# The whole program ordered by another simulation: timeline simulation in place of core simulation

## The chip, the cores and the metric

The kernel is one program on one core of a Trainium2 chip. The metric is the device time of one execution in microseconds (us), from the start of the program to its end. A core has five engines that run their own instruction lists in order and wait for one another through semaphores: TensorE (PE in the profile, its weight loads PEld), VectorE (DVE), ScalarE (ACT), GpSimd (POOL) and SyncE (SP), which here issues nearly all DMA transfers.

## The reference

The input is x, 256 tokens of 1024 features in float32, and one condition vector c of 1024. Cut to what matters:

```python
for i in range(2):                       # layer 0, layer 1
    shift, scale, gate = split(silu(c) @ ada_w[i] + ada_b[i], 3)
    h = rms_norm(x, norm_g[i]) * (1 + scale) + shift
    y = nsa_mixer(h, ...) if i == 0 else moba_mixer(h, ...)   # 16 heads of 64; (o * silu(z)) @ w_out
    x = x + gate * y
# second block: the same modulation; 8 heads of windowed attention and 8 heads of
# neighbourhood attention side by side, RMS norm of each half, w_out, gate, residual;
# then peer(): a router takes 8 x 16 of 16384 experts for each token,
# gelu(h . u_e) * softmax weight, summed over v_e; residual, final norm
```

## The kernel before

Everything is float32, held to float32 accuracy. A matrix product is written as three passes (`mm3`, L236): the left and right operand are split into a high and a low part, and high by high, high by low and low by high are summed in PSUM. A weight tile of 128x1024 is loaded by a DMA that SP issues (`raw`, four buffers), ScalarE casts each half to its high part (`hi`, L186) and VectorE subtracts to get the low part (`lo`, L211). A few tiles go into other buffers for the same purpose (`mo`).

The stages are: the first part of the modulation (`ada_first`, L350 on, its matmuls at L365); layer 0; layer 1 (both with scores L725, softmax L730 to L745, transposes of the probabilities L701, copies of them out of PSUM L703, products with v L706, and four units `z_unit` that compute the gate z); the second block (`block2`, L1135 on: `heads8` makes scores at L1117 and softmax at L1118 to L1131 for eight heads at once; `o_a` transposes at L1178 and multiplies at L1183, `o_b` at L1200 and L1206); and `peer`, which streams 128 tiles of u and 128 of v, two thirds of the time. `out_half` (L1251) multiplies the gated attention outputs (`ozh`, `ozl`) by w_out. Each layer begins with its norm: a row of small VectorE operations (`rstd_x`, L264) makes one factor for each token, a diagonal matrix of it is multiplied with x (`norm_x`, L517), and the projections follow.

The modulation of the later layers, `ada`, needs no attention at all: five groups a1 to a5 of 16 tiles of 512 KB, each tile two matmuls of 32x512 (L393) into one accumulator `psa`. The tiles have three buffers (`adaw`). These, the z units and the projections are the work that TensorE can do while an attention unit is in its softmax.

The program is written in the order of a string for each layer; `s` is a scores unit, `v` or `oa`/`ob` the transposes and products with v, `z` a gate unit, `a` an ada group, `o` and `O` the two halves of the output projection, and a number after `@` moves the priority of a step:

```python
'1': 'pA@1 q0 s000 s001 v00 q1@-2 s011 s010 v01@-4 z1 s100 z3 s110 s101 z0 z2 b s111 v10@-1 v11@-6 o O',
'2': 'pA@-2 qa@1 sa0 oa0 kb@-1 qb sa1 oa1 vb tb sb0@5 a4 ob0@1 sb1 a5 o ob1 O@5'
...
self.tc.cur_priority += 50 * int(later or 0)
f(*(int(c) for c in s[1:] if c.isdigit()))
self.tc.cur_priority -= 50 * int(later or 0)
```

This is not yet the order on the engines. The framework's scheduler (`TileContext`) simulates the program as it builds it, and gives each engine, among the instructions that are ready at that simulated time, the one of best priority; the buffers of the pools are handed out in the same pass. The resulting list of each engine is fixed in the program: on the chip an engine never overtakes an instruction that waits. For the last stage the code adds ordering of its own (`paced`, L1457).

## Time and profile before

| | |
|---|---|
| three runs | 1412.24, 1414.01, 1414.22 us; median 1414.01 us |
| profiled execution | 1413.74 us, of which the span of the trace is 1412.0 us |
| busy in the span | TensorE 1366.8, VectorE 1023.2, ScalarE 821.9, GpSimd 21.9 us |
| granted TensorE clock | 0.992 of 2.4 GHz on average |

TensorE is busy in 97% of the span. Its busy time contains matmuls that overlap, so groups of matmuls add up to more than the stretch they stand in; what is certain is the time in which it stood idle, about 45 us.

### The profile page before, as it was taken

Reading aid. Unit: us, or ns where it says so; the run is one execution under the profiler, and the core shown is the slowest. Engines: PE = TensorE matmul, PEld = TensorE weight load, DVE = VectorE, ACT = ScalarE, POOL = GpSimd, SP = SyncE. Lnnn points to the kernel's source line nnn. Section 1 sums busy time; section 2 is a strip of 40 time slices with the busy share of each in tenths; the row PEclk is TensorE's granted clock in tenths of the full one; section 3 lists DMA queues with packets and bytes.
Section 4 is the critical chain, followed back from the end, with each engine's and each line's share of the span. In section 5 each row is a group of like instructions: output and inputs, shape, how many; then the busy total and the mean of one; then the engine's idle time right before and its main releaser. Section 6 shows DMA issues by size and latency. Waiting matters only on the chain.

```text
span 1412.0 us, 24444 instructions
## 1 busy us (share of the span) xinstructions
PE 1366.8 (97%) x8522; PEld 1120.8 (79%) x8522; DVE 1023.2 (72%) x2636; ACT 821.9 (58%) x1887; POOL 21.9 (2%) x27
## 2 busy tenths in 40 slices
PE   6999999999989998999999999999999999999997
PEld 2566666477767755999999999999998888888885
DVE  3585756388665656799999968888866666677777
ACT  2353656357646654555555568888865555555554
POOL 0000000000001100000000000000000000000001
PEclk9999999999999999999999999999999999999999
DMA  8577564553486766455555555554456665677773
GB/s 309 199 272 273 197 203 138 199 186 101 138 313 199 216 225 223 135 182 179 179 179 179 181 188 193 165 164 162 165 194 227 194 194 194 194 227 239 245 242 114
DMA packets 94875, 279.15 MB, mean 198 GB/s; under 512 B 11112, under 2 KB 30320, under 8 KB 94624
## 3 DMA queue, kind: packets, MB, share of 16 engines
q1 hardware_dynamic: 94752, 277.59, 59.6%
q8 instruction: 67, 1.10, 0.3%
q14 instruction: 56, 0.46, 0.1%
HBM read 267.80 MB, written 13.94 MB: 200 GB/s over the span
## 4 chain that ended last, share of the span: by engine, by line
PE 90%; DVE 4%; DMA 4%; ACT 1%; issue 1%; SPq 0%; ACTq 0%; DVEq 0%
PE ps L240 18%; PE ps L239 18%; PE ps L241 18%; PE acc L240 5%; PE acc L239 5%; PE acc L241 5%; PE psa L393 5%; PE ps L1493 4%; PE ps L706 2%; DMA raw<-in_w1o 1%; PE ps L725 1%; PE ps L701 1%; PE psa L365 1%; DMA adaw<-in_adaw 1%; DVE lo L211 1%; PE ps L631 1%
## 5 line engine op out<-in xcount | busy, mean ns | idle before, releaser
L186 ACT CAST hi<-raw 128x512 fp32r<-128x512 f32 (+1 forms) x700 | 429.4, 618 | 349.9 <-PE ps L240 147.1
L211 DVE TENSOR_TENSOR lo<-raw,hi 128x512 fp32r<-128x512 f32 (+1 forms) x700 | 479.8, 688 | 179.7 <-ACT hi L186 162.8
L239 PE MATMUL ps<-hh,hi 128*128 128x256 f32 x1160 | 333.0, 287 | 1.3 <-DVE hh L187 1.3
L240 PE MATMUL ps<-hl,hi 128*128 128x256 f32 x1160 | 328.3, 283 | 1.1 <-DVE hl L211 1.1
L241 PE MATMUL ps<-hh,lo 128*128 128x256 f32 x1160 | 328.4, 283 | 0.0
L239 PEld LDWEIGHTS ps<-hh,hi 128*128 128x128 f32 x1160 | 222.6, 192 | 1.5 <-issue 1.5
L240 PEld LDWEIGHTS ps<-hl,hi 128*128 128x128 f32 x1160 | 222.4, 192 | 1.3 <-DVE hl L211 1.3
L241 PEld LDWEIGHTS ps<-hh,lo 128*128 128x128 f32 x1160 | 222.2, 192 | 0.0
L239 PE MATMUL ps<-hi,Ah 128*128 128x512 f32 x508 | 198.1, 390 | 0.0
L240 PE MATMUL ps<-lo,Ah 128*128 128x512 f32 x508 | 197.7, 389 | 0.0
L241 PE MATMUL ps<-hi,Al 128*128 128x512 f32 x508 | 197.6, 389 | 0.0
L239 PEld LDWEIGHTS ps<-hi,Ah 128*128 128x128 f32 x508 | 95.4, 188 | 20.1 <-issue 0.2
L241 PEld LDWEIGHTS ps<-hi,Al 128*128 128x128 f32 x508 | 95.4, 188 | 19.9
L240 PEld LDWEIGHTS ps<-lo,Ah 128*128 128x128 f32 x508 | 95.4, 188 | 19.9 <-DVE lo L211 0.2
L1492 ACT ACTIVATE og<-o,gT 128x128 f32<-128x128 bf16 x256 | 87.2, 394 | 4.1 <-DVE o L1490 0.3
L393 PE MATMUL psa<-adaw,cond 128*32 128x512 f32 x320 | 81.3, 610 | 3.1 <-DMA adaw<-in_adaw 3.1
L240 PE MATMUL acc<-lo,hh 128*128 128x512 f32 (+1 forms) x176 | 70.7, 402 | 2.4 <-DVE lo L211 2.4
L239 PE MATMUL acc<-hi,hh 128*128 128x512 f32 (+1 forms) x176 | 69.6, 401 | 2.6 <-DVE hh L187 1.4
L241 PE MATMUL acc<-hi,hl 128*128 128x512 f32 (+1 forms) x176 | 69.9, 398 | 0.0
L1493 PE MATMUL ps<-og,o 128*128 128x128 f32 x512 | 65.2, 275 | 0.1
L1493 PEld LDWEIGHTS ps<-og,o 128*128 128x128 f32 x512 | 61.4, 192 | 0.3 <-ACT og L1492 0.3
L733 ACT ACTIVATE P<-P,nm 128x128 f32<-128x128 f32 (+1 forms) x96 | 42.6, 446 | 13.5 <-DVE nm L730 13.4
(397 smaller groups left out, 1929.8 us busy)
## 6 DMA issues: line engine op xcount, KB each, us to landing
raw<-in_u SPq DMA_DIRECT2D x128, 512.0 KB, 3.6
raw<-in_v SPq DMA_DIRECT2D x128, 512.0 KB, 4.3
adaw<-in_adaw SPq DMA_DIRECT2D x86, 512.0 KB, 4.9
raw<-in_w SPq DMA_DIRECT2D x48, 512.0 KB, 4.3
raw<-in_wq SPq DMA_DIRECT2D x16, 512.0 KB, 3.4
zd<-ge SPq DMA_DIRECT2D x56, 128.0 KB, 1.7
ge<-zd SPq DMA_DIRECT2D x56, 128.0 KB, 3.6
raw<-in_adaw SPq DMA_DIRECT2D x10, 512.0 KB, 7.0
```

The costliest lines, as they stand in the source:

```text
L186: return self.nc.scalar.copy(out, in_)
L211: return self.nc.vector.tensor_tensor(lo, src, hi.bitcast(F32), op=OP.subtract)
L239: mm(out, a[0][asl], b[0][bsl], start=first, stop=False, **kw)
L240: mm(out, a[0][asl], b[1][bsl], start=False, stop=False, **kw)
L241: mm(out, a[1][asl], b[0][bsl], start=False, stop=last, **kw)
L365: nc.tensor.matmul(ps[32 * q:32 * q + 32], self.cond[:, k, :], raw[:, j * 512:(j + 1) * 512], start=(k == 0), stop=(k == NK - 1), tile_pos ...
L393: nc.tensor.matmul(ps[32 * q:32 * q + 32], self.cond[:, ci + k, :], raw[:, j * 512:(j + 1) * 512], start=(k == 0), stop=(k == NK - 1), til ...
L631: nc.tensor.transpose(pr[:P, i * 128:i * 128 + 128], s.rearrange("p a d -> p (a d)") if P == 128 else s, self.identr)
L706: nc.tensor.matmul(o[64 * a:64 * a + 64], v[br][kb][:, 2 * pair + a, :], pts[a], start=first, stop=False, tile_position=(0, 64 * a), skip_ ...
L733: nc.scalar.activation(Pb, Pb, AF.Exp, scale=-1.0, bias=nm[:, r, br:br + 1], accum_out=sums[:, r, br:br + 1])
L1492: nc.scalar.activation(og[:, j], o1[:, j], AF.Copy, scale=gT[:, t0 + j:t0 + j + 1])
L1493: nc.tensor.matmul(ps[:, j * 128:j * 128 + 128], o2[:, j], og[:, j], start=(j == 0), stop=(j == 3), skip_group_check=True)
```

## The change

The scheduler is told to take its simulated times from the framework's timeline simulation:

```diff
-    with tile.TileContext(nc) as tc:
+    with tile.TileContext(nc, schedule_with_timeline_sim=True) as tc:
```

No instruction is added or removed on any engine; what changes is the list of each engine, and with it the buffers that instructions get. In the last stage, from the router on, the lists of TensorE differ by a place or two. In the three layers ahead of it they differ widely. Three of the differences, in TensorE's lists (names with numbers are tiles; the number tells one tile from another of its kind):

First, the passage from layer 0 to layer 1. `acc_2529` is the last output product of layer 0, `ps_2784` the first product of the norm of layer 1, `psa_2675` the accumulator of an ada group. Before:

```order
L241 MATMUL acc_2529<-mo_2607,ozl1_2472 128x512
L239 MATMUL acc_2529<-mo_2611,ozh1_2315 128x512
L240 MATMUL acc_2529<-mo_2612,ozh1_2315 128x512
L241 MATMUL acc_2529<-mo_2611,ozl1_2472 128x512
L517 MATMUL ps_2784<-diag_2782,x0_86 128x128 x2
L393 MATMUL psa_2675<-adaw_2728,cond_82 32x512 x2
L517 MATMUL ps_2784<-diag_2782,x0_86 128x128 x2
L517 MATMUL ps_2789<-diag_2782,x0_86 128x128 x4
L393 MATMUL psa_2675<-adaw_2732,cond_82 32x512 x2
L393 MATMUL psa_2675<-adaw_2736,cond_82 32x512 x2
L239 MATMUL acc_2860<-hi_2862,hh_2771 128x512
L517 MATMUL ps_2827<-diag_2825,x1_87 128x128 x3
```

and in the changed program:

```order
L241 MATMUL acc_2529<-mo_2607,ozl1_2472 128x512
L239 MATMUL acc_2529<-mo_2611,ozh1_2315 128x512
L240 MATMUL acc_2529<-mo_2612,ozh1_2315 128x512
L241 MATMUL acc_2529<-mo_2611,ozl1_2472 128x512
L517 MATMUL ps_2784<-diag_2782,x0_86 128x128 x4
L517 MATMUL ps_2789<-diag_2782,x0_86 128x128 x4
L517 MATMUL ps_2827<-diag_2825,x1_87 128x128 x4
L517 MATMUL ps_2832<-diag_2825,x1_87 128x128 x4
L239 MATMUL acc_2860<-hi_2862,hh_2771 128x512
```

The ada tiles that stood before and among the norm's products are gone from here; they stand up to some 300 places earlier, inside layer 0's attention. The whole group a4, which stood in layer 1 and the second block, stands in layer 0 too, and its last tile goes ahead of layer 1.

Second, layer 1: scores `ps_3504` of an attention unit and the transposes (`P_3483` and so on) behind them. Before, the transposes and what stands around them:

```order
L239 MATMUL acc_3788<-hh_2771,hi_3791 128x256
L240 MATMUL acc_3788<-hl_2772,hi_3791 128x256
L393 MATMUL psa_5219<-adaw_5220,cond_82 32x512
L241 MATMUL acc_3653<-hh_2771,lo_3707 128x256
L239 MATMUL acc_3653<-hh_2771,hi_3706 128x256
L240 MATMUL acc_3653<-hl_2772,hi_3706 128x256
L241 MATMUL acc_3653<-hh_2771,lo_3707 128x256
L701 MATMUL ps_3516<-ident_85,P_3483 128x128
L701 MATMUL ps_3523<-ident_85,P_3451 128x128
L701 MATMUL ps_3516<-ident_85,P_3484 128x128
L701 MATMUL ps_3523<-ident_85,P_3452 128x128
L701 MATMUL ps_3516<-ident_85,P_3485 128x128
```

and in the changed program:

```order
L240 MATMUL acc_4054<-lo_4091,ozh0_2858 128x512
L241 MATMUL acc_4054<-hi_4090,ozl0_2859 128x512
L725 MATMUL ps_3499<-kT0_2851,qT_3155 128x256
L725 MATMUL ps_3499<-kT1_2852,qT_3155 128x256
L725 MATMUL ps_3504<-kT0_2851,qT_3155 128x256
L725 MATMUL ps_3504<-kT1_2852,qT_3155 128x256
L701 MATMUL ps_3516<-ident_85,P_3483 128x128
L701 MATMUL ps_3523<-ident_85,P_3451 128x128
L701 MATMUL ps_3523<-ident_85,P_3452 128x128
L701 MATMUL ps_3523<-ident_85,P_3453 128x128
L701 MATMUL ps_3523<-ident_85,P_3454 128x128
L701 MATMUL ps_3516<-ident_85,P_3484 128x128
```

The products of the z units (`acc_3653`, `acc_3788`: left `hh` and `hl`, L239 to L241, 128x256) stood between and behind the transposes. Now all four z units stand in one block ahead of layer 1's attention, and between the two groups of the last rows nothing is left but a third of the first output half (`acc_4054`).

Third, the second block: the second unit of the windowed attention, from its last scores (`qTa1`) over its transposes (`P8_4941`) to the products with v. Before:

```order
L239 MATMUL acc_5041<-hi_5088,hh_4252 128x512
L240 MATMUL acc_5041<-lo_5089,hh_4252 128x512
L241 MATMUL acc_5041<-hi_5088,hl_4253 128x512
L393 MATMUL psa_5219<-adaw_5256,cond_82 32x512 x2
L393 MATMUL psa_5219<-adaw_5260,cond_82 32x512
L1178 MATMUL ps_4997<-ident_85,P8_4941 128x128 x2
L1178 MATMUL ps_5004<-ident_85,P8_4941 128x128
L239 MATMUL acc_5040<-hi_5098,hh_4252 128x512
L1178 MATMUL ps_4997<-ident_85,P8_4941 128x128
L240 MATMUL acc_5040<-lo_5099,hh_4252 128x512
L1178 MATMUL ps_4997<-ident_85,P8_4941 128x128
L241 MATMUL acc_5040<-hi_5098,hl_4253 128x512
```

and in the changed program:

```order
L1117 MATMUL ps_4971<-kT0_4358,qTa1_4584 128x256
L1117 MATMUL ps_4971<-kT1_4359,qTa1_4584 128x256
L1178 MATMUL ps_4997<-ident_85,P8_4941 128x128 x2
L1178 MATMUL ps_5004<-ident_85,P8_4941 128x128
L1178 MATMUL ps_4997<-ident_85,P8_4941 128x128 x2
L1178 MATMUL ps_5004<-ident_85,P8_4941 128x128 x3
L1183 MATMUL ps_4996<-pt_5002,va0_4361 64x512
L1178 MATMUL ps_5013<-ident_85,P8_4941 128x128 x4
L1183 MATMUL ps_4996<-pt_5009,va0_4361 64x512
L1178 MATMUL ps_5020<-ident_85,P8_4941 128x128 x4
L1183 MATMUL ps_4996<-pt_5018,va1_4362 64x512
```

Before, 25 product passes (`acc_5040`, `acc_5041`, a projection) and three ada matmuls stood between the last scores and the first transposes of this unit, and more passes among the transposes; now there is nothing. The same holds for the two units of the neighbourhood attention behind it: of the ada group a5 (`psa_5397`), all 16 tiles now stand earlier, and what is left among these three units is 36 passes of the first output half and 24 of the second.

At the start of the program, in SP's list of DMA issues, the four loads of layer 0's first weight tiles stand at places 29, 33, 37 and 40 in place of 19 to 22; loads of the second ada half, of the constants (568 KB) and of the first tiles of a1 go ahead of them.

## Rows read from the trace of the kernel before

**Rows 1.** The profile's page: span, then each engine's busy time and instructions.
```profile
span 1412.0 us, 24444 instructions
...
PE 1366.8 (97%) x8522; PEld 1120.8 (79%) x8522; DVE 1023.2 (72%) x2636; ACT 821.9 (58%) x1887; POOL 21.9 (2%) x27
```

**Rows 2.** Busy time by stretch, whole run; the header names the columns.
```profile
core 0: us, PE busy (x) PEld busy (x) DVE busy (x) ACT busy (x) POOL busy (x), PEclk, DMA share, GB/s
0.00:30.00 30.00, 17.47 (x63) 6.76 (x64) 10.13 (x37) 10.27 (x23) 2.01 (x5) 0.91 0.90 315
30.00:60.00 30.00, 27.31 (x117) 14.73 (x116) 10.45 (x24) 6.53 (x14) 0.00 (x0) 0.97 0.61 204
60.00:210.00 150.00, 147.31 (x914) 98.05 (x913) 105.04 (x435) 77.80 (x203) 0.00 (x0) 1.00 0.69 238
210.00:300.00 90.00, 86.45 (x422) 51.39 (x421) 51.88 (x152) 43.29 (x106) 0.95 (x1) 0.98 0.50 172
...
318.00:390.00 72.00, 70.79 (x427) 53.34 (x425) 56.27 (x203) 49.95 (x133) 0.94 (x1) 1.00 0.37 125
390.00:420.00 30.00, 25.95 (x136) 18.24 (x135) 18.75 (x52) 14.10 (x34) 2.23 (x1) 1.00 0.82 295
...
476.00:550.00 74.00, 73.38 (x405) 40.55 (x403) 38.61 (x106) 42.81 (x108) 6.63 (x8) 1.00 0.73 232
550.00:562.00 12.00, 8.75 (x39) 6.83 (x38) 10.90 (x28) 5.13 (x11) 0.00 (x0) 0.95 0.46 153
562.00:575.00 13.00, 8.56 (x55) 8.23 (x56) 9.30 (x33) 5.48 (x13) 0.00 (x0) 0.78 0.42 148
575.00:1390.00 815.00, 814.92 (x5505) 755.91 (x5504) 644.33 (x1401) 510.55 (x1131) 0.00 (x0) 1.00 0.59 193
1390.00:1412.00 22.00, 12.14 (x53) 9.57 (x51) 14.06 (x35) 7.88 (x17) 3.88 (x3) 0.89 0.14 51
```

**Rows 3.** What TensorE waited for, 0 to 60 us.
```profile
PE psa L365 <- DMA adaw<-in_adaw: 5.9, 1, 5.9
PE psa L365 <- DMA raw<-in_adaw: 2.9, 2, 2.7
```

**Rows 4.** What TensorE waited for, 210 to 300 us.
```profile
PE ps L517 <- DVE diag L510: 1.1, 1, 1.1
```

**Rows 5.** What TensorE waited for, 550 to 575 us.
```profile
PE ps L517 <- DVE rx L274: 5.3, 1, 5.3
PE ps L239 <- DVE hh L187: 1.3, 1, 1.3
PE ps L240 <- DVE hl L211: 1.1, 1, 1.1
```

**Rows 6.** The chain that ended last, 0 to 60 us: start, length, what.
```profile
12.16 7.24 DMA raw<-in_adaw
...
25.41 0.57 issue
...
31.90 0.98 PE psa L365 x4
...
33.54 0.45 PE acc L241 x2
```

**Rows 7.** TensorE's groups by shape, 476 to 550 us: count, busy, mean ns, idle.
```profile
L393 PE MATMUL psa<-adaw,cond 128*32 128x512 f32 x92 | 24.0, 604 | 0.6 <-DMA adaw<-in_adaw 0.6
...
L1117 PE MATMUL ps<-kT,qTb 128*128 128x256 f32 x32 | 6.7, 289 | 0.0
L241 PE MATMUL acc<-hi,hl 128*128 128x512 f32 x15 | 6.1, 408 | 0.0
```

**Rows 8.** ScalarE's groups by shape, 476 to 550 us.
```profile
L1125 ACT ACTIVATE P<-P,nm 128x256 f32<-128x256 f32 x24 | 11.9, 499 | 6.0 <-DVE nm L1118 5.7 <-DVE nm L1121 0.3
L186 ACT CAST hi<-raw 128x512 fp32r<-128x512 f32 x16 | 9.6, 618 | 4.5 <-PE acc L241 4.5
L1131 ACT ACTIVATE P<-P,nm 128x256 f32<-128x256 f32 x18 | 7.6, 498 | 0.3 <-DVE nm L1128 0.3
L1202 ACT COPY pt<-ps 128x512 f32<-128x512 f32 x8 | 4.5, 586 | 10.9 <-PE ps L1200 10.9
L1125 ACT ACTIVATION_READ_ACCUMULATOR P<-P,nm 128x1 f32 x24 | 4.5, 187 | 0.0
```

**Rows 9.** ScalarE's groups by shape, 318 to 390 us.
```profile
L186 ACT CAST hi<-raw 128x512 fp32r<-128x512 f32 x27 | 16.4, 617 | 7.9 <-PE acc L241 4.0 <-PE acc L240 3.8
L733 ACT ACTIVATE P<-P,nm 128x256 f32<-128x256 f32 x16 | 8.0, 500 | 0.0
L703 ACT COPY pt<-ps 128x512 f32<-128x512 f32 x12 | 6.7, 584 | 6.4 <-PE ps L701 6.4
L733 ACT ACTIVATE P<-P,nm 128x128 f32<-128x128 f32 x16 | 6.3, 396 | 1.8 <-DVE nm L730 1.8
L733 ACT ACTIVATION_READ_ACCUMULATOR P<-P,nm 128x1 f32 x32 | 6.0, 189 | 0.0
```

## The prediction

> **What bounds the kernel now.** I read the page first: TensorE is busy in 1366.8 of 1412.0 us, VectorE in 1023.2, ScalarE in 821.9 [rows 1]. The kernel is bound by TensorE's work, and since the change neither adds nor removes an instruction, that work stays. What a new order can move is TensorE's idle time, 45 us. The table of stretches says where it lies [rows 2]: 15.2 us in the first 60 (busy 17.47 and 27.31 of 30 each), 2.7 us from 60 to 210, 3.6 from 210 to 300, 1.2 from 318 to 390, 4.1 from 390 to 420, 0.6 from 476 to 550, 7.7 from 550 to 575, 0.1 in the 815 us of the last stage, 9.9 in the tail. The last stage's lists are nearly the same, so its 815 us and the tail stay. The change acts in the first 575 us alone, where some 35 us of idle time can be won and any amount can be lost.
>
> How those 575 us came to be so full is seen in one row: from 476 to 550 us TensorE is busy 73.38 of 74 us, while ScalarE, at 42.81, and VectorE, at 38.61, do the softmax of three attention units [rows 2]. A softmax unit is a chain (scores, VectorE's maximum, ScalarE's exponentials, transposes, copies out of PSUM, products with v), and an engine cannot overtake a waiting instruction. What filled TensorE meanwhile was other work: ada matmuls, 92 records, and projection passes, three groups of about 15 like the one shown [rows 7].
>
> **The change part by part.** I price a stall as the chain's time on ScalarE less what TensorE still has in its list between the chain's ends. An ada tile (four records) takes 0.98 us, and two product passes of 512 columns 0.45 [rows 6], so 0.225 a pass. For scores and transposes I take at most 0.18 us, the mean of the 405 records in 73.38 us [rows 2].
>
> Second block: the three units from the second windowed one on. They now have no ada tile and no projection among them, so 92 x 0.245 = 22.5 us and 44 x 0.225 = 9.9 us leave; of the 73.4 us about 41 stay, with ten scores more about 42. ScalarE needs 24 exponentials with their sums at 0.499 + 0.187, 16.5 us; 18 scalings at 0.498, 9.0; 12 copies at 0.586, 7.0; 12 casts of weights at 0.618, 7.4; and nine smaller evacuations, priced like the copies, 5.3: 45 us [rows 8]. So ScalarE, not TensorE, is now the longer of the two, and they alternate. One unit's chain is 8 x 0.686 + 6 x 0.498 = 8.5 us. First unit: TensorE has 16 scores (2.9 us) and nothing more: 6 us idle. Second: 24 output passes (5.4 us) help, but four weight casts (2.5 us) stand among the exponentials: 8.5 + 2.5 - 2.9 - 5.4 = 3. Third: only two gate matmuls, some 1 us: 8.5 - 2.9 - 1 = 5. Together 14, less the 0.6 that is idle there now: **+13**. Below, if the scores and exponentials overlap better, +5; above, if the copies and products with v are exposed too (12 x 0.586), +20.
>
> Layer 1: the z units stand ahead of the attention, where they cover only the first scores. ScalarE's list from there to the last attention product is 16 wide and 8 narrow exponentials with 24 sums (8.0 + 3.2 + 4.5), 12 copies (7.0), 12 casts (7.4), and 14 others, scalings and evacuations, 7.4 by the same rows: 37.5 us [rows 9]. Eight heads: 8 x 0.689 + 1.0 for two scalings = 6.5 us against 16 scores and ten passes, 2.9 + 2.3: 1.3 idle, and 2 with VectorE's first step. The next sixteen: 17 us with four scalings and eight casts, against 32 scores (5.8) and 36 passes (8.1): 3. The last copies, with no filler behind them: 2. Together 7, less 1.2 idle now: **+6**, with bounds of 0 (VectorE is relieved by taking the z units away, and the first exponentials run beside the z block) and +14 (copies exposed).
>
> Layer 0 to layer 1: this passage is the one that I trust most, because the trace has it bare in another place. Between the second block and the last stage nothing covers the norm, and TensorE waits 5.3 us for the factor, then 1.3 and 1.1 for the first split operand [rows 5], 7.7 in all. Between layers 0 and 1 five ada tiles now cover it and the wait is 1.1 us [rows 4]. Without them: 7.7 - 1.1 = 6.6, and since 20 passes of the other token half follow in both places, I take **+6** (bounds +4 and +7). The passage from layer 1 to 2 had three ada tiles in its cover and has three of another group: 0.
>
> Layer 0: its attention keeps ada tiles among its units, those of a2 and a4, while its z units go ahead of them. It has 6.2 us idle in 60 to 300 [rows 2], and each tile must be loaded, with the DMA engines at 0.69 already in 60 to 210 [rows 2]. I take **+2**, between -4 (the present waits go) and +8 (an unfilled chain as in layer 1).
>
> Start: 12.5 us idle in the first 30 with the DMA share at 0.90 [rows 2]; the waits are for ada tiles, 5.9 and 2.9 us [rows 3], and the chain shows a transfer of 7.24 us from 12.16 on [rows 6]. The first weights now go behind more loads, which delays the first product; but more ada tiles can run while it waits. I take **+1**, between -8 and +6.
>
> Sum: 1 + 2 + 6 + 6 + 13 = 28, less 1 for waits on weights that the earlier loads may shorten: 27. On the profiled execution's 1413.7 us, 0.3 below the median of the three runs, that gives **1441 us**.
>
> The Trainium skill, Perfetto Trace Analysis, section Optimization Strategy, says that a kernel with several regimes, each with another most-contended engine, may gain by interleaving the regimes. This trace is such an interleaving by the row of 476 to 550 us, and the change takes part of it apart, so the rule speaks against it. Taken apart wholly, ScalarE's 45 and 37.5 us would stand against only the units' own TensorE work, by the row's mean of 0.18 for some 156 and 136 instructions 28 and 24 us: +31 for the two in place of +19, and 1453 us. I hold to the lists, which leave 60 and 48 output passes among these units.
>
> **The rivals.** Faster: the start. 15.2 us of idle time lie in the first 60 us. If what TensorE waits for there are loads that the new order brings earlier, or if the a1 tiles run in those waits, 10 us can be won, and where the attention units then lose under 7 the kernel gets faster: 1404 to 1410 us. For it speaks that ScalarE has only 42.81 of 74 us in the fullest attention stretch, so that exponentials may run ahead of their transposes; against it that the DMA share is 0.90 there, and that the first weights stand later.
>
> No change: the orders differ, but the engines' slack absorbs it, since ScalarE is at 58% over the span [rows 1]. The stalls would have to equal the present waits: 1411 to 1417 us. Between this and the forecast lies a small loss, 1417 to 1426, if each chain is half hidden.
>
> Slower than forecast: the clock. The stretch from 562 to 575 us has a granted clock of 0.78 after an idle stretch from 550 on, and the first 30 us 0.91 [rows 2]. A mean of 0.78 over 13 us is 5.7 us at 1.2 of 2.4 GHz, worth at most 2.9 us of work. If the four or five new stalls each draw this, 12 us come on top: 1453, and up to 1470 with the upper bounds of the terms. The Trainium skill, TensorE: Matmul & The Clock Gate, section HAM oscillation, describes such falls of the clock after idle gaps, and the trace agrees with it at 0.78 after the 550 us gap. Against it: from 390 to 420 us 4.1 us are idle and the clock stays at 1.00 [rows 2].
>
> **How the numbers follow.** The forecast's case, 1426 to 1453: 0.52. Beyond it by clock or larger stalls: 0.18. Small loss: 0.08. No change: 0.07. Faster: 0.15. The range reaches from the faster case's near end, 1408, to 1468 and leaves out about 0.15 at both ends; the forecast's own is 1426 to 1453. What a measurement of this kernel can tell from no change is about 0.2%, 3 us; by it faster 0.15, same 0.07, slower 0.78.
>
> **What would show it.** TensorE's busy sum within a few us of 1366.8, and the last stage's 815 us again full. A wait of about 5 us for the norm's factor at the passage from layer 0 to 1. Between the last scores and the first transposes of the second block's units, TensorE idle for 3 to 6 us each with ScalarE's exponentials or VectorE's rescaling as releaser, and ScalarE near full there. In layer 1 smaller gaps at the transposes. The prediction is wrong if these gaps are under 2 us, because the exponentials ran ahead; if the first 60 us shrink by more than 8; or if the last stage, which I took as unchanged, moves by more than 3 us.

## The result, and the profile after

The changed kernel takes 1488.62 us (median of four runs, 1487.99 to 1490.75) against 1413.96 us (1412.24 to 1414.22): 1.053 of the time before, with an interval of 1.0513 to 1.0547. That is 75 us slower where 27 were forecast, and beyond the range's upper end of 1468.

The page of the changed kernel, span and busy time of each engine, answers to [rows 1]:

```profile
span 1488.9 us, 24501 instructions
...
PE 1402.4 (94%) x8522; PEld 1141.2 (77%) x8522; DVE 1025.9 (69%) x2636; ACT 824.9 (55%) x1887; POOL 20.5 (1%) x27
```

The other engines' busy sums are what they were, and the 57 instructions more are all semaphore waits (2238 for 2181). TensorE has the same 8522 matmul records, but it is idle 41.3 us longer (86.5 against 45.2) and busy 35.6 us longer. Nearly half of the loss does not look like waiting at all; that is the first thing that the prediction's sum did not allow for.

To see where the loss lies I cut both runs at the same four events, the first norm product (L517) of the second half of layer 0's norm, and the first of layer 1, of the second block and of the last stage. Each row is a stage: start, layer 0, layer 1, second block, last stage; the columns are the length, each engine's busy time, the granted clock, the DMA share and GB/s. Before:

```profile
0.00:51.10 51.10, 37.77 (x144) 16.37 (x145) 13.58 (x42) 11.05 (x24) 2.01 (x5) 0.93 0.75 259
51.10:283.40 232.30, 224.38 (x1276) 142.04 (x1275) 150.97 (x568) 118.58 (x301) 0.95 (x1) 0.99 0.63 216
283.40:414.50 131.10, 125.42 (x699) 93.34 (x699) 100.81 (x334) 79.57 (x195) 3.17 (x2) 1.00 0.49 170
414.50:564.00 149.50, 143.63 (x796) 95.33 (x796) 92.05 (x241) 89.52 (x209) 11.90 (x16) 0.99 0.71 226
564.00:1412.00 848.00, 835.62 (x5610) 773.72 (x5610) 665.83 (x1454) 523.18 (x1158) 3.88 (x3) 1.00 0.58 188
```

and in the changed kernel:

```profile
0.00:53.20 53.20, 38.26 (x144) 18.40 (x145) 19.55 (x101) 11.38 (x25) 2.01 (x5) 0.87 0.86 300
53.20:318.10 264.90, 245.12 (x1361) 147.45 (x1360) 151.57 (x521) 122.38 (x305) 0.95 (x1) 0.97 0.63 222
318.10:459.70 141.60, 126.15 (x667) 94.50 (x667) 97.46 (x320) 78.45 (x191) 3.17 (x2) 0.93 0.39 129
459.70:636.10 176.40, 154.44 (x744) 104.56 (x744) 92.03 (x243) 90.40 (x209) 10.51 (x16) 0.89 0.47 150
636.10:1488.90 852.80, 838.45 (x5610) 776.27 (x5610) 665.30 (x1452) 522.29 (x1158) 3.82 (x3) 0.99 0.58 187
```

The lengths cannot be subtracted at once, since the change also moves ada matmuls from one stage to another: layer 0 has 38 more of them (128 for 90), layer 1 has 12 fewer and the second block 26 fewer. At 0.49 us each (half a tile of 0.98 us [rows 6], an estimate) that is 18.6, 5.9 and 12.7 us. With it taken out, the start lost 2.1 us, layer 0 14, layer 1 16.4, the second block 39.6 and the last stage 4.8; together 76.9, the difference of the spans. The second block is the worst: it has 52 records less to do, and TensorE is busy 10.8 us longer.

What TensorE waited for in the whole changed run answers to [rows 3 to 5]; the columns are total, times and longest, in us:

```profile
PE ps L517 <- DVE diag L510: 9.0, 2, 5.5
PE psa L365 <- DMA raw<-in_adaw: 6.1, 2, 3.2
PE psa L365 <- DMA adaw<-in_adaw: 5.8, 1, 5.8
PE ps L1178 <- DVE P L1133: 5.7, 1, 5.7
PE psa L393 <- DVE adar L400: 5.2, 1, 5.2
PE ps L517 <- DVE rx L275: 5.1, 1, 5.1
...
PE ps L1200 <- DVE P L1133: 2.7, 1, 2.7
```

Three of these are the stalls that the prediction named. L517 now waits 5.5 us at the passage from layer 0 to layer 1, where it waited 1.1 [rows 4]; the first transposes of the second block's units wait 5.7 us (L1178, forecast 6) and 2.7 us (L1200, forecast 3) for the rescaled probabilities `P`. The third unit, for which 5 us were forecast, has no gap of over 0.6 us; the timeline of TensorE says what stands there instead, between its last scores and its first transposes (start, busy, what):

```profile
606.57 3.62 PE L427 MATMUL ps<-adar,cst 128*128 128x512 f32 x4
609.98 1.06 PE L1200 MATMUL ps<-ident,P 128*128 128x128 f32 x4
```

These are the two gate matmuls that the prediction had at some 1 us. They took 3.62 us, 1.06 a record, where they took 1.88 before, 0.59 a record: the granted clock is 0.50 here, the lower level of 1.2 GHz, behind the second unit's waits.

One wait was not foreseen: 5.2 us for L400, ahead of the first tile of a5. The chain of work, at 438 us, says why (start, length, what):

```profile
438.69 1.15 SPq L398
...
440.92 10.80 DMA adar<-in_adab
451.75 0.05 DVEq L400
```

L400 adds the bias `adar` to the accumulator of a4 and frees `psa` for a5. All of a4's matmuls now stand in layer 0, but its bias cannot be loaded while the last user of the one `adar` buffer, an earlier gate, is still to come. So `psa` stays occupied through layer 1, which has no ada matmul from 273 to 452 us, until the bias has landed at 451.8. VectorE waits with it: L400 is next in its list, and behind it stand the last of the residual operations (L1274, L1275) and the norm's factor, although the output products that they take in had ended by 447.5. So a second wait follows, for the diagonal (start, busy, what, idle before):

```profile
451.84 0.69 DVE L400 TENSOR_TENSOR adar<-psa,adar 128x512 f32<-128x512 f32 x1 [8.26 <-DMA adar<-in_adab]
452.59 3.63 PE L393 MATMUL psa<-adaw,cond 128*32 128x512 f32 x12 [5.17 <-DVE adar L400]
459.68 5.58 PE L517 MATMUL ps<-diag,x 128*128 128x128 f32 x27 [3.46 <-DVE diag L510]
```

At this passage TensorE is idle for 8.6 us; before, it waited there 1.4 us for an ada tile and 0.8 for the factor.

### The profile page after: what moved, and what is told of

The parts are those of the page before. It is cut to its first block, busy times and chain, and to the rows that moved or that the text cites. A ratio compares the mean times of both kernels' runs of the same rounds, so it can differ in the third digit from the quotient of the medians.

```text
span 1488.9 us, 24501 instructions
## 1 busy us (share of the span) xinstructions
PE 1402.4 (94%) x8522; PEld 1141.2 (77%) x8522; DVE 1025.9 (69%) x2636; ACT 824.9 (55%) x1887; POOL 20.5 (1%) x27
## 4 chain that ended last, share of the span: by engine, by line
PE 86%; DMA 5%; DVE 4%; ACT 3%; SPq 1%; issue 1%; ACTq 0%; DVEq 0%
PE ps L240 17%; PE ps L239 17%; PE ps L241 17%; PE acc L239 6%; PE acc L240 5%; PE acc L241 5%; PE psa L393 4%; PE ps L1493 4%; PE ps L706 2%; DMA adaw<-in_adaw 2%; PE ps L701 1%; PE ps L725 1%; PE ps L517 1%; DMA raw<-in_adaw 1%; PE ps L631 1%; DMA adar<-in_adab 1%
## 5 line engine op out<-in xcount | busy, mean ns | idle before, releaser
L211 DVE TENSOR_TENSOR lo<-raw,hi 128x512 fp32r<-128x512 f32 (+1 forms) x700 | 480.5, 689 | 207.5 <-ACT hi L186 191.6
L239 PE MATMUL ps<-hh,hi 128*128 128x256 f32 x1160 | 333.7, 288 | 1.8 <-DVE hh L187 1.8
L241 PE MATMUL ps<-hh,lo 128*128 128x256 f32 x1160 | 329.0, 284 | 0.0
L239 PEld LDWEIGHTS ps<-hh,hi 128*128 128x128 f32 x1160 | 223.4, 193 | 2.8 <-DVE hh L187 2.0
L241 PEld LDWEIGHTS ps<-hh,lo 128*128 128x128 f32 x1160 | 222.9, 192 | 0.0
L241 PE MATMUL ps<-hi,Al 128*128 128x512 f32 x508 | 197.5, 389 | 0.0
L239 PE MATMUL ps<-hi,Ah 128*128 128x512 f32 x508 | 156.8, 389 | 0.0
L241 PEld LDWEIGHTS ps<-hi,Al 128*128 128x128 f32 x508 | 95.3, 188 | 20.0 <-issue 0.2
L239 PEld LDWEIGHTS ps<-hi,Ah 128*128 128x128 f32 x508 | 95.4, 188 | 19.7
L393 PE MATMUL psa<-adaw,cond 128*32 128x512 f32 x320 | 77.9, 621 | 9.5 <-DVE adar L400 5.2
L1492 ACT ACTIVATE og<-o,gT 128x128 f32<-128x128 bf16 x256 | 81.8, 391 | 3.8
L241 PE MATMUL acc<-hi,hl 128*128 128x512 f32 (+1 forms) x176 | 68.7, 390 | 0.4 <-DVE hl L211 0.4
L239 PE MATMUL acc<-hi,hh 128*128 128x512 f32 (+1 forms) x176 | 63.7, 398 | 1.5 <-ACT hh L186 1.0
L730 DVE CUSTOM_DVE_ANT_0 P<-ps,cst,qns 128x128 f32<-128x128 f32 (+1 forms) x96 | 35.3, 412 | 33.5 <-PE ps L725 33.2
```

The costliest lines, as they stand in the source:

```text
L211: return self.nc.vector.tensor_tensor(lo, src, hi.bitcast(F32), op=OP.subtract)
L239: mm(out, a[0][asl], b[0][bsl], start=first, stop=False, **kw)
L241: mm(out, a[1][asl], b[0][bsl], start=False, stop=last, **kw)
L393: nc.tensor.matmul(ps[32 * q:32 * q + 32], self.cond[:, ci + k, :], raw[:, j * 512:(j + 1) * 512], start=(k == 0), stop=(k == NK - 1), til ...
L730: vv.tensor_tensor_reduce(out=Pb, in0=ps[:, br * n:br * n + n].rearrange("p (a b) -> p a b", a=t + 1), in1=m2[:, 1 - t:2], scale=ns[:, h:h ...
L1492: nc.scalar.activation(og[:, j], o1[:, j], AF.Copy, scale=gT[:, t0 + j:t0 + j + 1])
```

## Where the longer busy time comes from

TensorE's list in the second windowed unit, from its first transposes on (start, busy, what, then the idle time before). In the changed kernel:

```profile
564.07 2.68 PE L1178 MATMUL ps<-ident,P 128*128 128x128 f32 x8 [5.73 <-DVE P L1133]
566.74 1.97 PE L1183 MATMUL ps<-pt,va 128*64 128x512 f32 x2
...
570.99 0.66 PE L1178 MATMUL ps<-ident,P 128*128 128x128 f32 x4
```

Before, around the same unit's transposes:

```profile
484.81 0.27 PE L1178 MATMUL ps<-ident,P 128*128 128x128 f32 x1
484.83 0.47 PE L239 MATMUL acc<-hi,hh 128*128 128x512 f32 x1
485.15 0.39 PE L240 MATMUL acc<-lo,hh 128*128 128x512 f32 x1
485.38 0.27 PE L1178 MATMUL ps<-ident,P 128*128 128x128 f32 x1
```

Before, a transpose of 0.27 us starts 0.02 us ahead of a product pass and lies beside it. In the changed kernel nothing lies beside them, and eight in a row count 2.68 us, 0.34 each. But the clock is lower there too. The granted clock is 0.50 from 560.09 us, within the wait, to 570.33, and 1.00 from then on, where four transposes in a row count 0.66 us, 0.17 each. The stretches at 0.50 in the second block of the changed kernel, four of six, and the sum of all six (columns as above):

```profile
459.70:464.52 4.82, 4.82 (x22) 4.82 (x23) 1.85 (x8) 1.51 (x4) 0.00 (x0) 0.50 1.04 332
...
560.09:570.33 10.24, 6.26 (x15) 2.68 (x16) 0.99 (x4) 7.14 (x23) 3.03 (x6) 0.50 0.61 103
590.81:597.64 6.83, 5.57 (x32) 3.94 (x31) 0.00 (x0) 2.87 (x7) 0.00 (x0) 0.50 0.07 26
601.05:611.29 10.24, 9.33 (x23) 5.41 (x22) 8.93 (x28) 8.47 (x27) 0.00 (x0) 0.50 0.32 102
...
sum 38.96, PE 32.82 PEld 22.51 DVE 17.43 ACT 23.27 POOL 3.03; mean PE 5.47 PEld 3.75 DVE 2.90 ACT 3.88 POOL 0.50
```

TensorE is busy there for 32.8 us at the lower level; before, at no time in the second block. Over the whole run it is 76.2 us, and 13.0 before. What runs at the lower level takes about 1.93 times as long (the four gate records, 3.62 us for 1.88), so of the 35.6 us that the busy sum grew some 30 are the clock (an estimate from these figures), and of the second block's 32.8 us the lower clock adds some 16. The transposes L1178 agree: they take 5.7 us before and 7.6 in the changed kernel, of which 3.8 at the lower level, and half of that with the rest gives 5.7 again.

What the clock leaves, some 5 of the 35.6 us, can be cover that was lost. The products with v (L706), grouped over the whole run, fit that. Before

```profile
L706 PE MATMUL ps<-pt,v 128*64 128x512 f32 x72 | 29.4, 619 | 0.0
```

and in the changed kernel

```profile
L706 PE MATMUL ps<-pt,v 128*64 128x512 f32 x72 | 40.7, 695 | 1.7 <-ACT pt L703 1.7
```

they differ by 11.3 us, and with 9.0 of the 40.7 us at the lower level the clock explains less than half of it.

ScalarE's groups of [rows 8] keep their durations, here from 541 to 636 us of the changed kernel; its exponentials did not become slower:

```profile
L1125 ACT ACTIVATE P<-P,nm 128x256 f32<-128x256 f32 x24 | 11.9, 499 | 6.0 <-DVE nm L1121 3.2 <-DVE nm L1118 2.8
```

So the second block lost 16.1 us in idle time and 23.5 in busy time, of which the lower clock accounts for some 16. A matmul that runs slower while the softmax is not ready need not make the block longer; what the clock costs in time is left to the experiments.

## The experiments

Three theories. **TensorE's list**: the cover taken out of TensorE's list is the loss, as predicted, only larger. **The other lists**: VectorE, ScalarE and SP were reordered as well, and delay what TensorE waits for. **The clock**: the gaps let the clock fall, and that is the cost. Most kernels pin the order of an engine to a table; `_hold` chains the instructions of a table by dependencies that order them and cost no semaphore:

```python
def _hold(nc, tc, order):
    by = {i.name: i for i in nc.cur_bb.bb.instructions}
    names = [f"I-{n}" for n in order if f"I-{n}" in by]
    for a, b in zip(names, names[1:]):
        tc.add_manual_dep(by[b], a, mybir.DependencyInfo(
            mybir.DependencyClass.NoSync, mybir.DependencyReason.DATA), reason="order of issue")
```

Tables are those of the kernel before unless it is said otherwise, and cover the three layers and what stands ahead of them. All kernels but the second start from the changed one.

A list left free is not the changed kernel's: the scheduler makes it anew around the pinned ones. By line, operation and tile names in the traces, 791 of VectorE's 1183 instructions of the layers stand in one common order before and in the changed kernel (the longest series that both lists have in the same order). The free VectorE list of e1 has 867 in common with the changed kernel's, that of e9 829; with e3, e4 and e8 it is 1056, 1097 and 1184. ScalarE's free list in e12 has 573 of 726 in common with the changed kernel's and 657 with that of before. So what a free list costs below is the cost of a list of the new scheduler, and not a share of the change's 75 us. Pinned lists are those of before, VectorE's but for some 26 places.

The table gives the ratio to the kernel before on the same chip, and the five stages in us, cut as above:

| kernel | ratio (interval) | start | layer 0 | layer 1 | second block | last |
|---|---|---|---|---|---|---|
| before | 1 | 51.1 | 232.3 | 131.1 | 149.5 | 848.0 |
| changed | 1.053 (1.0513 to 1.0547) | 53.2 | 264.9 | 141.6 | 176.4 | 852.8 |
| e1_pe_before | 1.0248 (1.0221 to 1.0276) | 57.4 | 237.5 | 143.6 | 156.3 | 851.3 |
| e2_pe_after | 1.0839 (1.0802 to 1.0876) | 47.3 | 307.9 | 148.9 | 178.5 | 847.7 |
| e3_ada_held | 1.0375 (1.0347 to 1.0403) | 53.2 | 249.7 | 140.2 | 173.3 | 850.9 |
| e4_block2_before | 1.031 (1.0274 to 1.0347) | 52.2 | 256.2 | 138.4 | 156.5 | 852.1 |
| e5_fill | 1.0582 (1.0535 to 1.0629) | 53.1 | 263.6 | 141.3 | 188.3 | 849.4 |
| e6_sp_free | 1.0074 (1.0037 to 1.0111) | 58.1 | 235.0 | 132.4 | 147.8 | 853.8 |
| e7_sp_before | 1.0151 (1.011 to 1.0192) | 50.8 | 235.3 | 142.7 | 157.2 | 851.4 |
| e8_fill_sized | 1.0507 (1.0476 to 1.0538) | 53.4 | 265.3 | 142.8 | 173.9 | 848.9 |
| e9_dve_free | 1.0136 (1.0106 to 1.0166) | 49.6 | 235.3 | 144.0 | 153.0 | 850.1 |
| e10_ada_free | 1.0319 (1.0277 to 1.0361) | 57.7 | 257.8 | 137.3 | 153.7 | 851.8 |
| e11_dve_act_before | 1.0729 (1.0681 to 1.0777) | 56.2 | 279.0 | 164.7 | 163.1 | 852.2 |
| e12_act_free | 1.011 (1.007 to 1.0151) | 52.4 | 235.7 | 135.8 | 153.2 | 851.6 |
| e13_layers_pinned | 1.0006 (0.9987 to 1.0025) | 50.3 | 230.8 | 130.4 | 148.3 | 850.9 |
| e14_all_pinned | 0.9988 (0.9972 to 1.0004) | 53.0 | 232.8 | 130.5 | 150.6 | 849.4 |

Each row's stages are those of one execution. e14 has the lists of before, and its stages differ from those of before by 0.5 to 1.9 us, so differences of 2 us between stages, and of 3 in the start, say nothing.

**TensorE's list alone put back: e1_pe_before.**

```diff
             Net(ctx, tc, a).run()
+            _hold(nc, tc, PE_ORDER)
```

> Changed scheduler, but TensorE's list of the three layers is pinned to the list of before; the lists of the other engines stay the changed scheduler's. If TensorE's list is the cause (theory 1), the idle time falls back to about 45 us, the clock to about 0.99, and the time to 1412 to 1425 us. If the other engines' lists (loads on SyncE, casts on ScalarE, steps on VectorE) are the cause (rival), TensorE waits for them all the same and the time stays above 1450 us.

1450.45 us. Some 40 of the 75 us come back, 35 stay, with TensorE's list exactly that of before in the three layers. So the list is a cause, and the lists that the new scheduler makes for the other engines around it are another. The second block is back from 176.4 to 156.3 us; the start is longer than in either parent, and layer 1 is still 12.5 us above before.

**TensorE's list alone changed: e2_pe_after.** The kernel before, its scheduler as it was, TensorE pinned to the changed kernel's list.

```diff
             Net(ctx, tc, a).run()
+            _hold(nc, tc, PE_ORDER)          # the table of the changed kernel
```

> The old scheduler, but TensorE's list of the three layers is pinned to the changed program's list; the lists of the other engines are the old scheduler's. Theory 1: 1470 to 1495 us, with the idle time and the clock of the changed kernel. Rival (other engines' lists): below 1440 us.

1534.96 us, worse than the change as a whole. TensorE waits 36.6 us for ada tiles, nine times, up to 12.6 us, and in layer 0 it is idle for 54.3 us. That its list asks for tiles in another order than the other lists bring them would explain it; this is not shown. A list cannot be judged apart from the other lists.

**The ada matmuls held back: e3_ada_held.** Each ada matmul is made to follow the instruction that it followed before; all else is left to the scheduler.

```diff
+            _hold(nc, tc, ADA_AFTER)         # (1560, 353), (1561, 353), ...
```

> Changed scheduler; only the ada matmuls may not go ahead of the attention instruction that they followed in the list of before. Layer 0 then holds 45 tiles again, layer 1 nine, the second block 26. The z units and projections stay in their blocks ahead of the attention. If the ada tiles are the larger part of the missing cover, the passages and the second block recover and the time is 1430 to 1455 us; if the z units and projections are, less than 20 us come back, 1468 to 1485 us.

1469.25 us: 0.0155 of 1415 us, 22 us, come back. With the ada matmuls in the second block again it is still 173.3 us long (26 matmuls more, so 16 us better like for like): the ada tiles were part of the cover, the product passes as large a part.

**The second block's TensorE list alone: e4_block2_before.** As e1, with the table cut to the second block.

```diff
+            _hold(nc, tc, PE_ORDER)          # 4266, 4267, ...
```

> Changed scheduler; TensorE's list of the second block alone, from its norm to the last stage, is pinned to that of before, which puts ten tiles of a4 back into it. By stage lengths, corrected for the ada tiles that changed stage, this block holds some 40 of the 75 us: theory 1 expects 1440 to 1455 us. If the second block is slow for what the layers ahead of it leave behind (buffers, loads), it stays above 1470 us.

1460.1 us: 31 us come back, and the second block takes 156.5 us as in e1. Its clock is 0.99 and its idle time 8.2 us (22.0 in the changed kernel). Of the 40 us that TensorE's list cost in all, this block has some 30.

**The gaps filled: e5_fill.** 40 ada-like matmuls with an output that nobody reads stand between the scores and the transposes of the units and ahead of the last norm.

```diff
+FILL = [(4973, 4998, 12), (5200, 5292, 8), (5481, 5597, 10), (5758, 5777, 10)]
+                mm = nc.tensor.matmul(ps[:32], self.cond[:, k % 8, :], self.cst[:, o:o + 512], ...)
```

> The changed kernel with 40 matmuls more, which nobody reads (32x512 float32, as an ada tile's, 0.49 us each, 19.6 us in all), put into TensorE's list at four places of the second block: 12, 8 and 10 between the last scores and the first transposes of its last three units, 10 ahead of the last stage's norm. They fill some 15 us of idle time and add about 5. If idle time is what takes the clock down (theory 1), the clock from 555 to 660 us goes from about 0.8 to near 1 and up to 20 us come back: 1470 to 1480 us, with more work. If the clock falls for another cause, the time is 1492 to 1500 us.

1499.12 us. The filler was larger than meant; all of it went to one place in PSUM and in TensorE's array (last section): the first group alone took 10.49 us for 24 records, so the 80 records some 35 us. The second block grew by 11.9 us, so 23 of the 35 us were hidden; its idle time fell from 22.0 to 7.5, its clock rose from 0.89 to 0.95. Too big to weigh the clock, so:

**The gaps filled with less: e8_fill_sized.** 24 such matmuls, over four places.

```diff
+FILL = [(4973, 4998, 10), (5200, 5292, 5), (5758, 5777, 9)]
+                mm = nc.tensor.matmul(ps[32 * (k % 4):32 * (k % 4) + 32], ...,
+                                      tile_position=(0, 32 * (k % 4)))
```

> The fill of the second block again, but sized to the gaps and spread over the four places of the accumulator as the ada matmuls are: 10 matmuls of 0.49 us behind the last scores of the second windowed unit, 5 behind those of the next unit, 9 ahead of the last stage's norm, 11.8 us against 13.5 us of idle time at these three places. If the fall of the clock behind the gaps costs time of its own, the run is 5 to 12 us faster than the changed kernel's 1489, at 1477 to 1484 us. If slower matmuls only wait less for the softmax, it is 1486 to 1492 us.

1487.5 us, the time of the changed kernel. The second block's stage:

```profile
461.50:635.40 173.90, 157.64 (x792) 103.07 (x792) 91.83 (x243) 90.25 (x209) 10.59 (x16) 0.93 0.46 152
```

Added work is hidden wholly, the clock is at 0.93 where it was 0.89, the stage 2.5 us shorter. But this filler came out smaller than meant: at 0.14 us a record (last section) its 48 records are some 6.7 us, and 16.3 us of idle time stay in the block. Of the 40 us at the lower clock it took 16 away. On that scale the whole fall would be worth some 6 us in the stage (an estimate, with the filler's own delay in it), and the medians differ by 1 us, which cannot be told from nothing. If every record at the lower level had held the block up, it would be the 16 us of above. By either figure the larger part of the block's 39.6 us is not the clock's; which of the two is nearer stays open, and layer 1, where the clock fell from 1.00 to 0.93, was not filled.

**TensorE, VectorE and ScalarE put back, SP free: e6_sp_free.**

```diff
+            _hold(nc, tc, PE_ORDER)
+            _hold(nc, tc, DVE_ORDER)
+            _hold(nc, tc, ACT_ORDER)
```

> Changed scheduler with the lists of TensorE, VectorE and ScalarE in the three layers pinned to those of before; only SyncE's list of loads is the changed scheduler's. Of the 34 us that were left with TensorE's list pinned alone, this shows the part of the loads: if the loads are the cause, about 1440 to 1450 us; if VectorE's and ScalarE's lists are, 1412 to 1422 us. At the start at least the first weights come later, so 3 to 6 us are expected of the loads by either.

1427.25 us, 10 us above before: 7 us in the start, 2.7 in layer 0, 1.3 in layer 1 and -1.7 in the second block. (The last stage's 853.8 us are in the profiled execution, the longest of its runs.) What TensorE waits for in its first 60 us answers to [rows 3]:

```profile
PE psa L365 <- DMA raw<-in_adaw: 7.7, 4, 3.6
PE psa L365 <- DMA adaw<-in_adaw: 6.1, 2, 5.8
```

The wait for the `raw` halves of the first modulation is 7.7 us where it was 2.9. The start takes 57.4 to 58.1 us in all three kernels that have TensorE's old list there and SP's new one (e1, e6, e10), and 49.6 to 53.0 in the five that have both old ones (e7, e9, e12, e13, e14).

**TensorE and SP put back: e7_sp_before**, and the same with **ScalarE too, VectorE free: e9_dve_free**, or **VectorE too, ScalarE free: e12_act_free.**

```diff
+            _hold(nc, tc, PE_ORDER)
+            _hold(nc, tc, SP_ORDER)
+            _hold(nc, tc, ACT_ORDER)         # e9 only; e12: DVE_ORDER
```

> Changed scheduler with TensorE's and SyncE's lists in the three layers pinned to those of before; VectorE's and ScalarE's are the changed scheduler's. The counterpart of the run before: 1412 to 1420 us if the loads made the 34 us, about 1440 us if VectorE's and ScalarE's lists did. The gaps at the norms (diagonal matrix, VectorE) and at the transposes of layer 1 stay in the second case.

> Changed scheduler with the lists of TensorE, SyncE and ScalarE in the three layers pinned to those of before; only VectorE's list is the changed scheduler's. With ScalarE's free too it was 22 us above the kernel before. If VectorE's list is the cause (steps of the norm's factor behind large operations and behind a wait for an ada group, splits late), 1430 to 1440 us; if ScalarE's is, 1414 to 1422 us.

> Changed scheduler with the lists of TensorE, SyncE and VectorE in the three layers pinned to those of before; only ScalarE's list is the changed scheduler's. By the run with VectorE's list free (1435 us) and that with both free (1438 us), ScalarE's list is worth 0 to 5 us: 1414 to 1421 us. This is also the measure of how well pinning gives the kernel before back: anything above 1425 us would say that something else than these lists, such as the buffers, costs time.

1438.11, 1434.68 and 1431.05 us: 21, 19 and 16 us above before. The last is above the 1425 us that were to point at something beside the lists, such as buffers; e13 and e14 below test that. They do not add up, since both lists together cost 21; and each is a list made anew. VectorE's free list costs 12.9 us in layer 1, ScalarE's 4.7 there, both together 11.6; in the second block they cost 3.5 and 3.7, together 7.7; in layer 0 each 3, and together 3.

One piece of what e9's VectorE list costs can be shown. The factor of the norm for layer 1's second token half is a row of small VectorE operations, L271 to L278, then the diagonal L510, for which TensorE's L517 waits. With e9's list (start, busy, what, idle before):

```profile
286.87 0.21 DVE L271 TENSOR_SCALAR rx<-ssx 128x1 f32<-128x1 f32 x1 [0.19 <-ACT acc L262]
...
289.25 0.69 DVE L400 TENSOR_TENSOR adar<-psa,adar 128x512 f32<-128x512 f32 x1 [1.35 <-PE psa L393]
...
290.26 0.68 DVE L211 TENSOR_TENSOR mo<-raw,mo 128x512 fp32r<-128x512 f32 x1
...
292.20 0.15 DVE L278 SCALAR_TENSOR_TENSOR rstd<-rx 128x1 f32<-128x1 f32 x1
...
293.54 0.28 DVE L510 TENSOR_SCALAR diag<-ident,rstd 128x128 f32<-128x128 f32 x1
```

and with its old one (e13, below):

```profile
282.62 0.21 DVE L271 TENSOR_SCALAR rx<-ssx 128x1 f32<-128x1 f32 x1
...
284.13 0.16 DVE L278 SCALAR_TENSOR_TENSOR rstd<-rx 128x1 f32<-128x1 f32 x1
...
285.28 0.28 DVE L510 TENSOR_SCALAR diag<-ident,rstd 128x128 f32<-128x128 f32 x1
285.47 0.69 DVE L400 TENSOR_TENSOR adar<-psa,adar 128x512 f32<-128x512 f32 x1
```

With the old list the row runs through, and the diagonal is there 2.7 us after its start. With e9's the ada step L400 stands in the middle of the row; VectorE itself waits 1.35 us there for TensorE's ada matmuls, and behind it three subtractions (L211, 0.68 each), a cast and four products of the first half (L532, 1.36) come ahead of the diagonal, 6.7 us after the start of the row. TensorE's waits in this place in e9 are 1.24 us for `hh` and 2.97 us for the diagonal, where the same places in e13 have none of over 0.5 us. That is 4.2 of the 12.9 us; later in the layer, gaps of 1.01, 1.62 and 0.84 us at the transposes (L701) stand against one of 0.68 us, for scores. TensorE's busy time in the layer is 5.0 us longer, at a granted clock of 0.96 after 1.00.

The changed kernel's own list does not have this piece, since its ada group stands elsewhere: the row of layer 1's second half takes 1.8 us there, from L271 at 316.97 to L510 at 318.77. It has the like in the row of the first half, which five splits (L211) and three residual operations (L1274, L1275) stretch to 6.0 us; before, with two of each, it took 3.7, from 274.81 to 278.51:

```profile
311.73 0.21 DVE L271 TENSOR_SCALAR rx<-ssx 128x1 f32<-128x1 f32 x1
...
317.75 0.28 DVE L510 TENSOR_SCALAR diag<-ident,rstd 128x128 f32<-128x128 f32 x1
```

TensorE's last output product starts at 312.15, and its 5.5 us of waiting for this diagonal fall into that row; the other place is L400 at the passage to the second block, shown above.

**TensorE put back but for the ada matmuls: e10_ada_free.**

```diff
+            _hold(nc, tc, PE_ORDER)          # without L393 and L410
```

> Changed scheduler; TensorE's list of the three layers is pinned to that of before for everything but the ada matmuls, which the changed scheduler places: 64 tiles in layer 0, 6 in layer 1, 10 in the second block. The counterpart of the run with the ada matmuls held. With all pinned it was 1450 us, with only the ada matmuls held 1469. If the ada tiles are a separate loss of some 20 us, 1465 to 1475 us; if they only matter where z units and projections are gone as well, 1450 to 1458 us.

1460.03 us, 10 us above e1. Where the scheduler puts the ada tiles is worth 10 us with the rest of TensorE's list in place and 22 us without (e3).

**VectorE and ScalarE put back, TensorE and SP free: e11_dve_act_before.**

```diff
+            _hold(nc, tc, DVE_ORDER)
+            _hold(nc, tc, ACT_ORDER)
```

> Changed scheduler with the lists of VectorE and ScalarE in the three layers pinned to those of before; TensorE's and SyncE's lists are free, and the scheduler makes them anew around the pinned ones. The counterpart from the other side: if VectorE's list is a loss of its own of some 19 us and TensorE's order one of its own, 1465 to 1475 us; if a good VectorE list also brings TensorE's list right, below 1445 us; if lists of two schedulers disturb one another, above 1489 us.

1517.8 us, 29 us above the changed kernel. With e2 this is the second mixture of two schedules that is worse than both.

**All four lists put back in the layers, e13_layers_pinned, and every list in the whole program, e14_all_pinned.**

```diff
+            _hold(nc, tc, PE_ORDER)
+            _hold(nc, tc, SP_ORDER)
+            _hold(nc, tc, DVE_ORDER)
+            _hold(nc, tc, ACT_ORDER)
+            _hold(nc, tc, POOL_ORDER)        # e14 only, where the tables cover the last stage too
```

> Changed scheduler with all four lists (TensorE, SyncE, VectorE, ScalarE) of the three layers pinned to those of before; the last stage is free. If the lists of the layers are the whole loss and each of the last runs (one list free: 1427, 1435, 1431 us) shows that list's own part, this is 1412 to 1419 us. If some 10 us stay, the last stage's lists or the buffers are a part that all pinned runs carried, and the parts of the single lists are that much smaller.

> Changed scheduler with the lists of all five engines pinned to those of before over the whole program. The lists are then those of before, and only what the scheduler decides beside them (buffers, semaphores) can differ: 1412 to 1419 us if nothing there matters, and the difference to the run before is the part of the last stage's order.

1416.73 and 1414.13 us, both the time of before. In e14's trace the lists of TensorE, VectorE, ScalarE and SP are those of before from end to end, by line, operation and tile names. With the lists of the layers put back nothing is left to explain, neither by buffers, which the new scheduler still hands out, nor by the last stage. The lists of the layers, taken together, are the whole loss.

## Why the prediction was wrong

The direction was right, and the mechanism, cover taken out of TensorE's list, is about half of the loss. By the prediction's own steps:

1. **"I price a stall as the chain's time on ScalarE less what TensorE still has in its list."** This is the step that failed first. It takes the order of the other engines' lists as given: apart from SP's start and four casts among ScalarE's exponentials, no term asks in which order they do their work. With TensorE's list as it was, the new scheduler's lists for the other engines cost 35 us (e1). In the changed kernel itself the place that shows it is the passage to the second block (4). I had their order before me as I had TensorE's, and looked at one engine because the page said that it is the bound.

2. **Second block, +13: mis-sized.** It measured +39.6, of which some 30 are TensorE's list (e4); free lists of VectorE and ScalarE cost 7.7 there (e7). The gaps in the first two units came as priced, 5.7 for 6 and 2.7 for 3, and idle time grew by 16.1. But the third unit's wait showed no gap, since its scores and gate matmuls ran at the lower clock and the latter took 3.62 us of it, not 1; and 23.5 us of the loss stand in TensorE's busy time.

3. **"That work stays", and a busy sum within a few us of 1366.8.** It grew by 35.6. The records stayed, but 76.2 us of them ran at the lower clock, where 13.0 did before, which is some 30 of the 35.6 (an estimate). Both bounds of the term (5 and 20) were made of idle time, and the clock stood apart from it as a rival. With TensorE's old list in the block (e4) its busy time there is 148.3 us with 52 more records, against 154.4, and the granted clock 0.99.

4. **Layer 1, +6, and the passage from layer 1 to 2, 0: +16.4 together.** The passage is the part that is seen: 8.6 us idle for 2.2. I compared the ada tiles in its cover, three and three, and did not read that their accumulator `psa` still needs a bias whose buffer an earlier gate holds, nor that VectorE's list puts L400 ahead of the additions and the factor. How the rest of layer 1 splits is not shown: a VectorE list of the new scheduler costs 12.9 us there (e9), but it is not the changed kernel's.

5. **Passage from layer 0 to 1, +6: right in kind.** The wait is 5.5 us for 1.1. With it, layer 0's +2 and +6 make 8; it measured 14. With TensorE's list put back layer 0 is 5.2 us above before (e1), so its list has about 9 of them.

6. **Start, +1: +2.1, within its bounds,** and not to be told from nothing, since kernels with the old lists have 49.6 to 53.0 us there. But not because little hangs on it: with TensorE's old list SP's new order costs 7 us there (e6). The two changed lists fit each other.

7. **Last stage, 0.** Its 4.8 us, beyond the 3 that were named as a sign of being wrong, are not the change's: with the new scheduler's own order in it the stage is 848.9 us in e8 and 849.4 in e5, with every list put back 849.4.

8. **The clock's rival, +12.** The clock did fall, to 0.89 in the second block, and stretched TensorE's work by some 30 us in all. What that cost in time is not settled: less of the lower clock gave back 2.5 us in e8, and the second block's share is between some 6 and 16 us. Beside it stand the "larger stalls" of the same line, and its 1470 was too low as well.

9. **The rule on interleaving regimes** (the Trainium skill, Perfetto Trace Analysis, section Optimization Strategy) spoke against the change, and the measurement agrees; the 1453 us that came out by it were nearer than my sum, for the same reason too low: it also took the order of the other engines' lists as given.

What stays open: how the loss outside the second block splits among the engines' lists, and that of e7 into single places; how much of the loss is the lower clock and how much the waits themselves; why the timeline simulation takes these orders for good ones; and what a second `adar` buffer would give, for which there is no run.

## What to carry to other kernels

Where a scheduler gives every engine a new list, the lists are one thing: read the order of each engine around the few values that the bounding engine waits for (a norm's factor, a bias that frees an accumulator), and don't price the bounding engine's list alone; putting back TensorE's alone won 40 us here, putting back VectorE's and ScalarE's lost 29. The idle time of the bounding engine is no ceiling for a loss and its busy sum no constant: 76 us of its matmuls ran at the lower clock and took nearly twice as long. To find out whose list it is, pin lists to those of the faster kernel in combinations, and first all of them together, which shows whether anything else is left to look for. A scheduler makes the lists that are left free anew, so compare them with those of the kernel in question before you give them a share of its loss.

## What the runs showed of the hardware

Matmuls of one shape differ threefold in what a row of them takes. In e5 all fillers wrote the same 32 rows of PSUM from the same place in the array (`tile_position`), in e8 they went round four places of 32 in both; the first group of each between the same two instructions, e5

```profile
557.06 10.49 PE L1592 MATMUL psf<-cst,cond 128*32 128x512 f32 x24
```

and e8

```profile
558.94 2.77 PE L1592 MATMUL psf<-cst,cond 128*32 128x512 f32 x20
```

take 0.44 and 0.14 us a record, though a record by itself lasts 0.59 us and the granted clock is 1.00 in both. Whether the place in PSUM or that in the array does it is not separated here. The rows of [rows 6], 0.98 us for four, lie between at 0.245.

The granted clock can be low where TensorE shows few gaps. From 590 to 610 us of the changed kernel, from the second unit's first transposes to the third unit's, it is 0.61 while TensorE is busy 17.18 of 20 us:

```profile
590.00:610.00 20.00, 17.18 (x77) 11.08 (x78) 8.92 (x29) 13.38 (x37) 0.00 (x0) 0.61 0.22 75
```

A mean of 0.61 is most of the stretch at 1.2 of 2.4 GHz. Before, from 390 to 420 us, 25.95 of 30 us busy left it at 1.00 [rows 2]. Why the lower level was granted here and not there, these runs do not tell. What it does to the reading they do: the third unit's stall is in the profile as slow gate matmuls and not as a gap, so that idle time, by which the prediction meant to check itself, misses it.
